# Advancing a state-space scan four time steps at a time instead of two, in a two-layer decoder trunk

## The chip, the cores and the metric

The kernel runs on one core of a Trainium2 chip. The metric is the time of one execution on the device in microseconds. The core has a matrix engine (TensorE, PE in the profile; its weight loads have a row of their own, PEld), a vector engine (VectorE, DVE), a scalar engine (ScalarE, ACT), GpSimd (POOL) and SyncE (SP), which here issues the loads. Each engine takes its instructions in the order of its own queue, and they wait for one another by semaphores. Matmuls write PSUM; everything else lives in SBUF.

## The reference

Batch 1, 256 positions, model width 2048, float32. Layer 0 normalises x, projects it, and splits the result into `xa`, `ga` (1024 channels each) and `zb`, `gb` (2048 and 1024). The part that matters here is the state-space mixer on `xa`: 64 groups of 16 channels, each with 64 complex states.

```python
    ab_re = mag * jnp.cos(li * dt)
    ab_im = mag * jnp.sin(li * dt)
    ...
    bu_re = jnp.einsum('blgh,gph->blgp', uf, bb_re)
    bu_im = jnp.einsum('blgh,gph->blgp', uf, bb_im)
    ...
    _, _, h_re, h_im = lax.associative_scan(combine, (a_re, a_im, bu_re, bu_im), axis=1)
    y = (jnp.einsum('blgp,ghp->blgh', h_re, c_re.astype(f32))
         - jnp.einsum('blgp,ghp->blgh', h_im, c_im.astype(f32))
         + d_skip.astype(f32)[None, None] * uf)
```

So h(t) = a h(t-1) + bb u(t) for each state, and y(t) = Re(C h(t)) + d u(t). After it come a GELU, a gated linear unit (`w_glu`), and a product with silu(`ga`). The other half of layer 0 is a spatial gate on `zb`, `gb`; both halves go through `w_out0`, and x is added. Layer 1 is differential attention with its own projections; a last normalisation follows.

## The kernel before

**Weights and main matmuls.** All weight matrices are cut into 140 chunks of 512 rows by 512 columns. SP loads them in a fixed order, written out by hand (`stream`), three buffers ahead. Each chunk is split in two exact parts: ACT writes the rounded part `wh` (line 82, the helper for all ACT work), DVE the rest `wl` (line 61, the helper for elementwise work on two tensors), again with three buffers. Three matmuls (hi by hi, hi by lo, lo by hi) take the place of one: `gemm_t` with 512 moving columns (lines 208 to 210), `gemm_c` with 256 (lines 221 to 224). Splits and the evacuation of a finished result are marked high priority. A planner that simulates engines in time orders the rest, in general by the order in which the program states it; the order of SP alone is kept as written. Main results have two PSUM buffers; the side work has one of two banks (`side2`) and two of one bank (`side1`, lanes 0 and 1).

**The state-space side work.** Groups are taken in pairs, so that 32 input channels and 128 states (2 x 64) belong together; there are 32 pairs. Time is taken two steps at a time: h(t+1) = a^2 h(t-1) + (a bb u(t) + bb u(t+1)), so 128 block steps remain of 256 positions. The steps are these:
- `ssm_params`: from the parameters dt, |a|, the phase, a (`ab`), the input factor (`fc`), its product with a (`fa`), |a|^2 (`r2`) and the powers of the unit rotation.
- `e_tables(half)`: for 16 pairs, a table E of the rotation's powers, 128 columns, by doubling.
- `ssm_consts`: `bbr` (the input matrices bb and a bb), `cA` and `cN` (output matrices C a and C), spread by masked copies into zeroed tiles, for all 32 pairs at once; and `pk0`, the direct path from u(t) to y(t), added to a diagonal of d (`diag_skip`, on POOL) in `intra`.
- `ssm_bT`: the input matrices transposed by TensorE (`pbt`) into `bT`.
- `ssm_set(S)`, 8 sets of 4 pairs: W = bT u (line 568), turned back by E (`f`), scanned on DVE with the real factor r2 (line 584, one scan for each pair and part), turned forward (`b`, then `hst`), and y from `hst` through `cA` and `cN` (line 606) plus `intra` (line 598); for every second set GELU into `yaf`.

These are generators: `run_side` advances them between chunks of the `v` matmuls, the constants run before `xa`, the sets of a half follow `xa` of that half in program order, ahead of `u`, `gb` and `ga`. Their result is needed at `glu`, after the first half of `w_out0` (`eo`). `yaf` is split there into `yah` and `yal`.

**In float32**, a matmul stands in the profile as two records, each with a weight load of its own; a transpose as one.

Of the kernel before, what the change touches and what calls it, by code (L numbers as in the profile page):

```python
# [29 lines left out]
def hybrid_trunk_kernel(ctx: ExitStack, tc: tile.TileContext, xT, xtok, w_in0, w_glu, w_out0,  # L30
# [53 lines left out]
    def rsqrt_mean(name, ss, n, eps, post=None):  # L84
        """(ss / n + eps) ** -0.5: an integer first guess, a cubic step and a Newton step."""
# [32 lines left out]
    # ---------------------------------------------------------------- weight stream  # L118
# [37 lines left out]
    def split(upto, before=None):  # L156
        """hi = the weight rounded to float32r, lo = the exact rest."""
# [80 lines left out]
    # ---------------------------------------------------------------- start: x^T, norm  # L238
# [51 lines left out]
    # the norm's factor: per token on partitions, and as a row on every partition  # L290
# [31 lines left out]
    # ---------------------------------------------------------------- SSM constants  # L322
# [34 lines left out]
    cst = {}  # L357

    def ssm_params():
# [7 lines left out]
        r2 = p32("r2")  # L367
        mul(r2, mag, mag)
        cst["r2"] = r2
# [50 lines left out]
        fa = p32("fa", 64).rearrange("p (c m) -> p c m", c=2)  # L420
        mul(t1, fc[:, 0, :], ab[:, 0, :])
        mul(t2_, fc[:, 1, :], ab[:, 1, :])
        sub(fa[:, 0, :], t1, t2_)
        mul(t1, fc[:, 0, :], ab[:, 1, :])
        mul(t2_, fc[:, 1, :], ab[:, 0, :])
        add(fa[:, 1, :], t1, t2_)
        cst.update(ab=ab, fc=fc, fa=fa, ep=ep)
        yield
        # powers of exp(i * 2 phi): 1, 2, 4, ..., 64
        pw = []  # L430
        prev = ep
        for j in range(7):
# [5 lines left out]
            e = p32(f"pw{j}", 64).rearrange("p (c m) -> p c m", c=2)  # L438
# [5 lines left out]
        cst["pw"] = pw  # L444
        yield

    bbr = [None, None]

    def sc16(ap):
        return ap.unsqueeze(2).to_broadcast([128, 32, 16])  # L450

    def diag_skip():
        intra = t8(11, "intra", [128, 16, 128])
        for i in range(16):
            G.tensor_scalar(out=intra[:, i, :], in0=ident, scalar1=dq[:, i:i + 1], scalar2=None, op0=ALU.mult)
        cst["intra"] = intra

    def masked(dst, src):
        for gg in range(2):
            r = slice(gg * 64, gg * 64 + 64)  # L460
            act(dst[r, :, gg * 16:gg * 16 + 16], src[r], AF.Copy)

    def ssm_consts():
        for c in range(2):
            bbr[c] = t8(7 + c, f"bbr{c}", [128, 32, 2, 32])
            G.memset(bbr[c], 0.0)
        cA = t8(9, "cA", [128, 2, 32, 32])
        cN = t8(10, "cN", [128, 2, 32, 32])
        G.memset(cA, 0.0)
        G.memset(cN, 0.0)  # L470
        cst.update(cA=cA, cN=cN)
        b_re, b_im, c_re, c_im = (bct[:, i] for i in range(4))
        for gg in range(2):
            r = slice(gg * 64, gg * 64 + 64)
            h = slice(gg * 16, gg * 16 + 16)
            act(cN[r, 0, :, h], c_re[r], AF.Copy)
            act(cN[r, 1, :, h], c_im[r], AF.Copy, scale=-1.0)
        yield
        for key, z_re, z_im, o_re, o_im, sign in (
                ("fc", b_re, b_im, bbr[0][:, :, 1, :], bbr[1][:, :, 1, :], 1.0),  # L480
                ("fa", b_re, b_im, bbr[0][:, :, 0, :], bbr[1][:, :, 0, :], 1.0),
                ("ab", c_re, c_im, cA[:, 0], cA[:, 1], -1.0)):
            s = cst[key]
            m1 = t4(f"m1{key}", [128, 2, 32, 16])
            m2 = t4(f"m2{key}", [128, 2, 32, 16])
            mul(m1[:, 0], z_re, sc16(s[:, 0, :]))
            mul(m1[:, 1], z_im, sc16(s[:, 1, :]))
            mul(m2[:, 0], z_im, sc16(s[:, 0, :]))
            mul(m2[:, 1], z_re, sc16(s[:, 1, :]))
            sub(m1[:, 0], m1[:, 0], m1[:, 1])  # L490
            if sign > 0:
# [3 lines left out]
            masked(o_re, m1[:, 0])  # L495
            masked(o_im, m2[:, 0])
            yield
        # K0 = Re(C bb) and the skip, as one matrix per two pairs
        intra = cst["intra"]
        pk0 = side1("pk0", [128, 16, 32])  # L500
        for i in range(16):
            for q in range(2):
                P = i * 2 + q
                o = pk0[q * 64:q * 64 + 32, i, :]
                PE.matmul(o, bbr[0][:, P, 1, :], cN[:, 0, P, :], start=True, stop=False)
                PE.matmul(o, bbr[1][:, P, 1, :], cN[:, 1, P, :], start=False, stop=True)
        for q in range(2):
            r = slice(q * 64, q * 64 + 32)
            o = intra[r, :, q * 64:q * 64 + 32]
            add(o, pk0[r], o)  # L510
        yield

    def ssm_bT():
        bT = [t8((14, 6)[c], f"bT{c}", [128, 16, 128]) for c in range(2)]
        for c in range(2):
            for g in range(4):
                p = side1(f"pbt{c}{g}", [128, 4, 128], g % 2)
                for ct in range(4):
                    i = g * 4 + ct
                    src = bbr[c][:, 2 * i:2 * i + 2].rearrange("p q j h -> p (q j h)")  # L520
                    PE.matmul(p[:, ct, :], src, ident, start=True, stop=True, is_transpose=True)
                act(bT[c][:, g * 4:g * 4 + 4, :], p, AF.Copy)
            yield
        cst["bT"] = bT

    U2 = t8(12, "U2", [128, 2, 2, 4, 128])
    etab = {}

    def e_tables(half):
        E = big.tile([128, 2, 16, 128], F32, name=f"E{half}", tag="e")  # L530
        etab[half] = E
        hs = slice(half * 16, half * 16 + 16)
        pw = cst["pw"]
        V.memset(E[:, 0, :, 0:1], 1.0)
        V.memset(E[:, 1, :, 0:1], 0.0)
        V.tensor_copy(out=E[:, :, :, 1:2], in_=pw[0][:, :, hs].unsqueeze(3))
        for k in range(1, 7):
            n = 1 << k
            for q in range(2):
                ph = slice(q * 8, q * 8 + 8)  # L540
                es = E[:, :, ph, 0:n]
                sh = [128, 8, n]
                m = [t4(f"em{half}{k}{q}{i}", [128, 2, 8, 64])[:, :, :, 0:n] for i in range(2)]
                for i in range(2):
                    a = pw[k][:, i, half * 16 + q * 8:half * 16 + q * 8 + 8].unsqueeze(2).to_broadcast(sh)
                    for c in range(2):
                        mul(m[i][:, c], es[:, c], a)
                o = slice(n, 2 * n)
                sub(E[:, 0, ph, o], m[0][:, 0], m[1][:, 1])
                add(E[:, 1, ph, o], m[0][:, 1], m[1][:, 0])  # L550
# [574 lines left out]
```

## Time and profile before

| | |
|---|---|
| median of 3 runs | 888.91 us (888.35 to 889.16) |
| profiled execution, its span | 887.3 us |
| PE / DVE / ACT / POOL busy | 871.7 / 666.3 / 448.8 / 38.3 us |
| first `xa` result evacuated (`xs`) | 101.7 us |
| last `yaf` copy starts | 307.4 us |
| first matmul of `glu` | 335.0 us |
| granted TensorE clock, mean | 0.996 |

The span runs from the first to the last instruction of one profiled execution; the times of the runs are the device's for a whole execution, so a little more than the span (here 1.6 us between the median and the span, which are of different executions). Busy shares are averages over stages; a PE that is busy can still be slower than its best, since the ends of matmuls are modelled and overlap the next.

### The profile page before, as it was taken

The page shows a single profiled execution, that of the slowest core. Times are in us where ns is not written, and L with a number is a line of the kernel's source. Part 1 is how long each engine was busy: PE and PEld are TensorE (multiplying, and loading weights), DVE is VectorE, ACT ScalarE, POOL GpSimd, SP SyncE. Part 2 cuts the span into 40 slices and gives each one's busy share as a digit, 9 for nine tenths or more (in the row PEclk, how much of TensorE's full clock was granted, in tenths as well). Part 3 has the DMA queues.
Part 4 walks back from the last instruction along what each step waited for, and adds up shares of the span by engine and source line. Part 5 has one row for each costly group of instructions (what it writes and reads, how often), then busy time and mean ns, then how long its engine had stood idle before and what let it go on. Part 6 is the DMA issues. An engine that isn't in the chain of part 4 may idle for free.

```text
span 887.3 us, 14016 instructions
## 1 busy us (share of the span) xinstructions
PE 871.7 (98%) x5598; PEld 778.4 (88%) x5598; DVE 666.3 (75%) x1219; ACT 448.8 (51%) x623; POOL 38.3 (4%) x47
## 2 busy tenths in 40 slices
PE   9999999999999999999999999999999999999995
PEld 7799978788999789889988999889988998888895
DVE  8999869999988866567866677666767577665773
ACT  6563862455334645565345543554346544554551
POOL 7110000000000100000000000000000000000000
PEclk9999999999999999999999999999999999999998
DMA  8965452234534655455554545554454455555542
GB/s 306 379 243 191 143 190 96 96 120 166 190 114 141 259 185 176 170 195 202 180 182 160 188 145 190 191 190 152 181 190 171 165 188 196 183 189 190 178 155 96
DMA packets 25985, 160.24 MB, mean 181 GB/s; under 512 B 2880, under 2 KB 4160, under 8 KB 7744
## 3 DMA queue, kind: packets, MB, share of 16 engines
q1 hardware_dynamic: 25344, 156.20, 49.2%
q0 software_dynamic: 576, 3.15, 1.0%
q8 instruction: 44, 0.72, 0.3%
q14 instruction: 21, 0.17, 0.1%
HBM read 157.24 MB, written 2.10 MB: 180 GB/s over the span
## 4 chain that ended last, share of the span: by engine, by line
PE 90%; DVE 7%; ACT 1%; issue 1%; DMA 0%; DVEq 0%; ACTq 0%
PE v L209 5%; PE v L210 5%; PE v L208 5%; PE k L224 3%; PE q L221 3%; PE k L223 3%; PE k L221 3%; PE q L224 3%; PE q L223 3%; PE g L210 3%; PE g L209 3%; PE g L208 3%; PE od L209 2%; PE od L208 2%; PE od L210 2%; PE ga L221 2%
## 5 line engine op out<-in xcount | busy, mean ns | idle before, releaser
L82 ACT ACTIVATE wh<-wr 128x1024 fp32r<-128x1024 f32 (+1 forms) x276 | 288.7, 1047 | 356.0 <-PE v L210 64.0
L61 DVE TENSOR_TENSOR wl<-wr,wh 128x1024 fp32r<-128x1024 f32 (+1 forms) x276 | 331.8, 1205 | 142.2 <-ACT wh L82 141.4
L224 PE MATMUL k<-h2h,wl 128*128 128x256 f32 x256 | 72.8, 284 | 0.0
L221 PE MATMUL q<-h2h,wh 128*128 128x256 f32 x256 | 72.7, 284 | 0.0
L223 PE MATMUL q<-h2l,wh 128*128 128x256 f32 x256 | 72.7, 284 | 0.0
L224 PE MATMUL q<-h2h,wl 128*128 128x256 f32 x256 | 72.6, 284 | 0.0
L221 PE MATMUL k<-h2h,wh 128*128 128x256 f32 x256 | 72.4, 283 | 0.0
L223 PE MATMUL k<-h2l,wh 128*128 128x256 f32 x256 | 72.4, 283 | 0.0
L209 PE MATMUL v<-wl,h2h 128*128 128x512 f32 x128 | 50.8, 397 | 0.0
L209 PE MATMUL g<-wl,h2h 128*128 128x512 f32 x128 | 50.3, 393 | 0.0
L210 PE MATMUL g<-wh,h2l 128*128 128x512 f32 x128 | 50.1, 391 | 0.0
L210 PE MATMUL v<-wh,h2l 128*128 128x512 f32 x128 | 50.0, 390 | 0.0
L208 PE MATMUL v<-wh,h2h 128*128 128x512 f32 x128 | 50.0, 390 | 0.0
L208 PE MATMUL g<-wh,h2h 128*128 128x512 f32 x128 | 49.9, 390 | 0.0
L224 PEld LDWEIGHTS k<-h2h,wl 128*128 128x128 f32 x256 | 49.1, 192 | 0.1
L221 PEld LDWEIGHTS q<-h2h,wh 128*128 128x128 f32 x256 | 49.1, 192 | 0.2
L221 PEld LDWEIGHTS k<-h2h,wh 128*128 128x128 f32 x256 | 49.1, 192 | 0.0
L223 PEld LDWEIGHTS k<-h2l,wh 128*128 128x128 f32 x256 | 49.1, 192 | 0.0
L223 PEld LDWEIGHTS q<-h2l,wh 128*128 128x128 f32 x256 | 49.1, 192 | 0.0
L224 PEld LDWEIGHTS q<-h2h,wl 128*128 128x128 f32 x256 | 49.1, 192 | 0.0
L209 PE MATMUL od<-wl,oh 128*128 128x512 f32 x96 | 37.6, 392 | 0.0
L208 PE MATMUL od<-wh,oh 128*128 128x512 f32 x96 | 37.5, 391 | 0.0
(331 smaller groups left out, 2182.8 us busy)
## 6 DMA issues: line engine op xcount, KB each, us to landing
wr<-in_w_in_dram SPq DMA_DIRECT2D x100, 1024.0 KB, 4.8
wr<-in_w_out_dram SPq DMA_DIRECT2D x32, 1024.0 KB, 4.8
wr<-in_w_glu_dram SPq DMA_DIRECT2D x4, 1024.0 KB, 4.7
wr<-in_w_in_dram SPq DMA_DIRECT2D x8, 256.0 KB, 4.5
wr<-in_w_in_dram SPq DMA_DIRECT2D x4, 512.0 KB, 7.9
xk<-in_xtok_dram SPq DMA_DIRECT2D x2, 1024.0 KB, 10.9
xr<-in_xtok_dram POOLq DMA_DIRECT2D x2, 1024.0 KB, 7.6
out_dram<-x SPq DMA_DIRECT2D x6, 256.0 KB, 2.6
```

Source lines behind the costliest of these rows:

```text
L61: (eng or V).tensor_tensor(out=o, in0=a, in1=b, op=op)
L82: A.activation(out=o, in_=i, func=f, **kw)
L208: PE.matmul(ps[:, t, :], hi[:, s], wh, start=first and a == 0, stop=False)
L209: PE.matmul(ps[:, t, :], hi[:, s], wl, start=False, stop=False)
L210: PE.matmul(ps[:, t, :], lo[:, s], wh, start=False, stop=last and a == len(ktiles) - 1)
L221: PE.matmul(ps[:, c, :], wh[:, s], hi, start=first and a == 0 and c % 2 == 0, stop=False, skip_group_check=True)
L223: PE.matmul(ps[:, c, :], wh[:, s], lo, start=False, stop=False, skip_group_check=True)
L224: PE.matmul(ps[:, c, :], wl[:, s], hi, start=False, stop=fin, skip_group_check=True)
```

## The change

Time is taken four steps at a time. With a^4 (`r4`) as the factor of the scan, 64 block steps remain. Each pair's four inputs of 32 channels fill all 128 rows (`U`), in the order of steps 3, 2, 1, 0. The input matrices are a^k bb for k = 0 to 3 (`bbr`, from `sB`), the output matrices C a^(i+1) for the four outputs i (`ccs`, from `sC`). The outputs come from the state with which a block begins (`hst`, whose first column stays zero) and from a block matrix `intra` of 128 rows by 128, made of the products C a^k bb (`pk`, `kx`, transposed to `kt`) and the diagonal d.

The sets become 4 of 8 pairs. E has 64 columns; one scan takes all 8 pairs of a part in a row of 512, with a factor table `R` that is zero at the first column of each pair. The constants are built for one set at a time (`ssm_bc(s)`, `ssm_mats(s)`): for set 0 where they stood before, for sets 1 to 3 between the sets. `bbr`, `ccs`, `intra` and `cN` are one tile each, written anew for each set; `bT` is a new tile in one place. Places change: `bbr` goes from places 7 and 8 to 9, `ccs` to 10, `intra` and `cN` with the factors to 11. The input copies of `xs` into `U` are 16 for each half, of 256 columns, where 8 of 512 were. `rsqrt_mean`, the main matmuls and layer 1 are the same; some comments are gone.

```diff
@@ ssm_params
-        r2 = p32("r2")
-        mul(r2, mag, mag)
+        r4 = p32("r4")
+        mul(r4, mag, mag)
+        mul(r4, r4, r4)
...
+        sB, sC = (ic[:, z:z + 256].rearrange("p (c k m) -> p c k m", c=2, k=4) for z in (1536, 1792))
+        def cmul(o, x, y, n):
+            yb = [y[:, c].unsqueeze(1).to_broadcast([128, n, 32]) for c in range(2)]
+            m = t2("cm", [128, 2, n, 32])
+            for c in range(2):
+                mul(m[:, 0], x[:, 0], yb[c])
+                mul(m[:, 1], x[:, 1], yb[1 - c])
+                (add if c else sub)(o[:, c], m[:, 0], m[:, 1])
+        V.tensor_copy(out=sC[:, :, 0], in_=ab)
+        V.tensor_copy(out=sB[:, :, 0], in_=fc)
+        cmul(sC[:, :, 1:2], sC[:, :, 0:1], ab, 1)
+        cmul(sC[:, :, 2:4], sC[:, :, 0:2], sC[:, :, 1], 2)
+        cmul(sB[:, :, 1:4], sC[:, :, 0:3], fc, 3)
...
-    def diag_skip():
-    def ssm_consts():
-    def ssm_bT():
...
+    bbr = t8(9, "bbr", [128, 2, 8, 4, 32])
+    ccs = t8(10, "cc", [128, 2, 8, 4, 32])
+    intra = ic[:, 0:1024].rearrange("p (m i h) -> p m i h", m=8, i=4)
+    cN = ic[:, 1024:1536].rearrange("p (c m h) -> p c m h", c=2, m=8)
...
+    def ssm_zero():
+        for z in (ic[:, 0:1536], bbr, ccs):
+            G.memset(z, 0.0)
...
     def masked(dst, src):
         for gg in range(2):
             r = slice(gg * 64, gg * 64 + 64)
+            act(dst[r, :, :, gg * 16:gg * 16 + 16].rearrange("p m k h -> p k m h"), src[r], AF.Copy)
+    def ssm_bc(s):
+        if not s:
+            ssm_zero()
+        ms = slice(s * 8, s * 8 + 8)
+        b_re, b_im, c_re, c_im = (bct[:, i, ms] for i in range(4))
+        for gg in range(2):
+            r, h = slice(gg * 64, gg * 64 + 64), slice(gg * 16, gg * 16 + 16)
             act(cN[r, 0, :, h], c_re[r], AF.Copy)
             act(cN[r, 1, :, h], c_im[r], AF.Copy, scale=-1.0)
+        sh = [128, 4, 8, 16]
+        for key, z_re, z_im, o in (("sB", b_re, b_im, bbr), ("sC", c_re, c_im, ccs)):
...
+            mul(m1[:, 0], z_re, f_re)
+            mul(m1[:, 1], z_im, f_im)
+            mul(m2[:, 0], z_im, f_re)
+            mul(m2[:, 1], z_re, f_im)
             sub(m1[:, 0], m1[:, 0], m1[:, 1])
...
+            masked(o[:, 0], m1[:, 0])
+            masked(o[:, 1], m2[:, 0])
             yield
+    def ssm_mats(s):
+        pk = side1(f"pk{s}", [128, 2, 128], 1)
+        for g in range(2):
+            for r in range(4):
+                for c in range(2):
+                    PE.matmul(pk[r * 32:r * 32 + 32, g], cN[:, c, g * 4 + r, :],
+                              bbr[:, c, g * 4 + r].rearrange("p k h -> p (k h)"), start=c == 0, stop=c == 1,
+                              skip_group_check=True)
+        kx = t2(f"kx{s}", [128, 2, 128])
+        act(kx[:, :, 32:128], pk[:, :, 32:128], AF.Copy)
+        for g in range(2):
+            stt(kx[:, g, 0:32], i32, d4[:, s * 2 + g:s * 2 + g + 1], pk[:, g, 0:32], ALU.mult, ALU.add)
+        yield
+        bT = t8(14, f"bT{s}", [128, 2, 8, 128])
         for c in range(2):
+            for g in range(2):
+                p = side1(f"pbt{s}{c}{g}", [128, 4, 128], g)
+                for r in range(4):
+                    PE.matmul(p[:, r, :], bbr[:, c, g * 4 + r].rearrange("p k h -> p (k h)"), ident,
+                              start=True, stop=True, is_transpose=True)
+                act(bT[:, c, g * 4:g * 4 + 4, :], p, AF.Copy)
             yield
+        kt = side1(f"kt{s}", [128, 8, 32], 1)
+        for g in range(2):
+            PE.matmul(kt[:, g * 4:g * 4 + 4].rearrange("p m h -> p (m h)"), kx[:, g], ident,
+                      start=True, stop=True, is_transpose=True)
+        for i in range(4):
+            k = 3 - i
+            for r0, n in ((0, 128),) if k == 0 else ((0, 64),) if k == 2 else tuple((r, 32) for r in range(0, 128 - 32 * k, 32)):
+                act(intra[r0 + 32 * k:r0 + 32 * k + n, :, i], kt[r0:r0 + n], AF.Copy)
+        yield
...
     def e_tables(half):
+        if not half:
+            E[0] = big.tile([128, 2, 32, 64], F32, name="E", tag="e")
...
-        for k in range(1, 7):
+        for k in range(1, 6):
...
+    def ssm_set(s):
...
+        W = side2(f"W{s}", [128, 2, 8, 64])
         for c in range(2):
+            for m in range(8):
+                PE.matmul(W[:, c, m, :], cst["bT"][:, c, m, :], U[:, s * 8 + m, :], start=True, stop=True)
+        R = t2(f"R{s}", [128, 8, 64])
+        r4 = cst["r4"][:, ms].unsqueeze(2)
+        act(R[:, :, 0:1], r4, AF.Copy, scale=0.0)
+        act(R[:, :, 1:64], r4.to_broadcast([128, 8, 63]), AF.Copy)
...
         for c in range(2):
+            gf = flat(g)[:, c]
+            V.tensor_tensor_scan(out=gf, data0=R.rearrange("p m t -> p (m t)"), data1=gf, initial=0.0,
+                                 op0=ALU.mult, op1=ALU.add)
...
+        sub(h[:, 0, :, 1:64], m1[:, 0, :, 0:63], m2[:, 1, :, 0:63])
+        add(h[:, 1, :, 1:64], m1[:, 1, :, 0:63], m2[:, 0, :, 0:63])
         yield
+        y = side1(f"y{s}", [128, 8, 64], 1)
+        for m in range(8):
+            PE.matmul(y[:, m, :], intra[:, m].rearrange("p i h -> p (i h)"), U[:, s * 8 + m, :],
+                      start=m == 0, stop=False, skip_group_check=True)
+        for m in range(8):
+            for c in range(2):
+                PE.matmul(y[:, m, :], ccs[:, c, m].rearrange("p i h -> p (i h)"), h[:, c, m, :],
+                          start=False, stop=c == 1, skip_group_check=True)
...
+        for q in range(2):
+            for i in range(4):
+                r = slice((qh * 2 + q) * 32, (qh * 2 + q) * 32 + 32)
+                o = ya["f"][r, half * 4:half * 4 + 4, :].rearrange("p c (t i) -> p c i t", i=4)[:, :, i, :]
+                act(o, y[i * 32:i * 32 + 32].rearrange("p (c q) t -> p q c t", q=2)[:, q], AF.Gelu_apprx_tanh)
...
     def ssm_half(half):
         if half:
             yield from e_tables(half)
+        for s in (2 * half, 2 * half + 1):
+            if s:
+                yield from ssm_bc(s)
+                yield from ssm_mats(s)
+            yield from ssm_set(s)
     side.append(ssm_params())
     side.append(e_tables(0))
-    side.append(ssm_consts())
+    side.append(ssm_bc(0))
...
-    for _ in ssm_bT():
+    for _ in ssm_mats(0):
         pass
...
             for q4 in range(4):
-                for j in range(2):
+                for j in range(4):
+                    r0 = (3 - j) * 32
...
```

## Rows read from the trace of the kernel before

**Rows 1.** The page, busy time of each engine, its share of the span, instructions
```profile
PE 871.7 (98%) x5598; PEld 778.4 (88%) x5598; DVE 666.3 (75%) x1219; ACT 448.8 (51%) x623; POOL 38.3 (4%) x47
```

**Rows 2.** The table of windows: us, then each engine's busy us, clock, DMA
```profile
100.00:200.00 100.00, 96.60 (x589) 79.69 (x588) 86.65 (x174) 52.41 (x69) 0.00 (x0) 1.00 0.35 123
200.00:310.00 110.00, 109.64 (x782) 98.07 (x781) 98.08 (x144) 53.18 (x60) 4.10 (x7) 1.00 0.48 172
310.00:870.00 560.00, 560.00 (x3459) 504.79 (x3458) 382.00 (x580) 280.33 (x407) 8.22 (x10) 1.00 0.50 178
```

**Rows 3.** Waits of PE: on whom, us in total, times, longest
```profile
PE v L209 <- DVE wl L61: 1.6, 2, 0.8
PE gb L208 <- ACT ut L82: 1.4, 1, 1.4
...
PE u L209 <- DVE wl L61: 0.8, 1, 0.8
PE pbt L521 <- ACT bT L82: 0.8, 1, 0.8
PE u L208 <- ACT ut L82: 0.5, 1, 0.5
```

**Rows 4.** Groups of PE: form, passes, busy us, mean ns
```profile
L568 PE MATMUL W<-U,bT 64*128 64x128 f32 x128 | 17.2, 281 | 0.0
L606 PE MATMUL y<-hst,cA 128*32 128x128 f32 x128 | 16.4, 274 | 0.0
```

**Rows 5.** Chain of waits, 90 to 310 us: start us, us, piece
```profile
99.26 0.59 PE pbt L521 x4
...
177.54 0.34 PE y L606 x2
...
179.66 1.88 PE y L606 x30
...
195.22 1.98 PE W L568 x16
...
202.87 0.89 PE y L598 x8
...
275.32 1.09 PE y L598 x8
```

**Rows 6.** Tile pk, line 506: ns min/median/max, first and last start us
```profile
L506 PE MATMUL pk<-cN,bbr x64: 196/196/217, 97.0 to 99.1; 128*32 128x32 f32 x64
```

**Rows 7.** Timeline at 419 us: start us, us, instruction
```profile
418.77 0.28 PE L224 MATMUL q<-h2h,wl 128*128 128x256 f32 x1
418.77 0.31 PEld L841 LDWEIGHTS plam<-lprod,ones 128*128 128x128 f32 x2
418.89 0.28 PE L841 MATMUL plam<-lprod,ones 128*128 128x2 f32 x2
419.00 0.19 PEld L221 LDWEIGHTS q<-h2h,wh 128*128 128x128 f32 x1
...
419.23 0.28 PE L223 MATMUL q<-h2l,wh 128*128 128x256 f32 x1
```

**Rows 8.** Groups of DVE: form, count, busy us, mean ns
```profile
L584 DVE TENSOR_TENSOR_SCAN f<-r,f 128x128 f32<-128x128 f32 x64 | 21.1, 401 | 0.0
...
L61 DVE TENSOR_TENSOR em<-E,pw 128x512 f32<-128x512 f32 x16 | 10.1, 683 | 0.0
```

**Rows 9.** Groups of ACT: form, count, busy us, mean ns
```profile
L82 ACT ACTIVATE U<-xs 32x512 f32<-32x512 f32 x16 | 10.5, 658 | 0.6 <-DVE xs L61 0.4
...
L82 ACT ACTIVATE x2s<-x 128x256 f32<-128x256 f32 x4 | 1.7, 417 | 14.6 <-DVE x L61 14.6
...
L82 ACT ACTIVATE bbr<-m1fc 64x512 f32<-64x512 f32 x2 | 1.2, 622 | 0.0
```

**Rows 10.** Tile yaf, its reader yal: ns min/median/max, first and last start us
```profile
L61 DVE TENSOR_TENSOR yal<-yaf,yah x2: 1220/1223/1226, 288.7 to 310.3; 128x1024 fp32r<-128x1024 f32 x2
```

**Rows 11.** Tile glu, its first matmuls, columns as in the group before
```profile
L221 PE MATMUL glu<-yah,wh x64: 277/283/283, 335.0 to 357.7; 128*128 128x256 f32 x64
```

More of the change, by code (lines that the diff above doesn't have):

```diff
@@ L443, in ssm_params @@
             prev = e
[L444 removed]
+        cst["pw"] = pw[1:]
         yield
[L447 to L456 removed]
+    bbr = t8(9, "bbr", [128, 2, 8, 4, 32])
+    ccs = t8(10, "cc", [128, 2, 8, 4, 32])
+    intra = ic[:, 0:1024].rearrange("p (m i h) -> p m i h", m=8, i=4)
+    cN = ic[:, 1024:1536].rearrange("p (c m h) -> p c m h", c=2, m=8)
+    d4 = const.tile([128, 8], F32, name="d4")
+    i32 = const.tile([128, 32], F32, name="i32")
+    def ssm_zero():
+        for z in (ic[:, 0:1536], bbr, ccs):
+            G.memset(z, 0.0)
+        for r in range(4):
+            q = r % 2
+            rows = slice(r * 32, r * 32 + 32)
+            act(d4[rows], dq[q * 64:q * 64 + 32].rearrange("p (g a) -> p a g", a=2)[:, r // 2], AF.Copy)
+            act(i32[rows], ident[rows, rows], AF.Copy)
     def masked(dst, src):
@@ L511, in ssm_consts @@
         yield
-    def ssm_bT():
-        bT = [t8((14, 6)[c], f"bT{c}", [128, 16, 128]) for c in range(2)]
+        bT = t8(14, f"bT{s}", [128, 2, 8, 128])
         for c in range(2):
[L516 to L522, printed above, removed]
+            for g in range(2):
+                p = side1(f"pbt{s}{c}{g}", [128, 4, 128], g)
+                for r in range(4):
+                    PE.matmul(p[:, r, :], bbr[:, c, g * 4 + r].rearrange("p k h -> p (k h)"), ident,
+                              start=True, stop=True, is_transpose=True)
+                act(bT[:, c, g * 4:g * 4 + 4, :], p, AF.Copy)
@@ L537, in e_tables @@
-        for k in range(1, 7):
+        V.memset(e[:, 0, :, 0:1], 1.0)
+        V.memset(e[:, 1, :, 0:1], 0.0)
+        V.tensor_copy(out=e[:, :, :, 1:2], in_=pw[0][:, :, hs].unsqueeze(3))
+        for k in range(1, 6):
             n = 1 << k
[L539 to L550, printed above, removed]
+            m = [t4(f"em{half}{k}{i}", [128, 2, 16, n]) for i in range(2)]
+            for i in range(2):
+                a = pw[k][:, i, hs].unsqueeze(2).to_broadcast([128, 16, n])
+                for c in range(2):
+                    mul(m[i][:, c], e[:, c, :, 0:n], a)
+            o = slice(n, 2 * n)
+            sub(e[:, 0, :, o], m[0][:, 0], m[1][:, 1])
+            add(e[:, 1, :, o], m[0][:, 1], m[1][:, 0])
@@ L551, in e_tables @@
             if k >= 4:
                 yield
[L553 to L575 removed]
+    ya = {}
@@ L608, in ssm_set @@
-        yield
-        if q == 1:
-            if "f" not in ya:
-                ya["f"] = t8(7, "yaf", [128, 8, T])
-            for qq in range(2):
-                for i in range(2):
-                    r = slice((qh * 2 + qq) * 32, (qh * 2 + qq) * 32 + 32)
-                    o = ya["f"][r, half * 4:half * 4 + 4, :].rearrange("p c (t i) -> p c i t", i=2)[:, :, i, :]
-                    act(o, y[qq * 64 + i * 32:qq * 64 + i * 32 + 32], AF.Gelu_apprx_tanh)
+        y = side1(f"y{s}", [128, 8, 64], 1)
@@ new lines, in ssm_set @@
+        for m in range(8):
+            PE.matmul(y[:, m, :], intra[:, m].rearrange("p i h -> p (i h)"), U[:, s * 8 + m, :],
+                      start=m == 0, stop=False, skip_group_check=True)
+        for m in range(8):
+            for c in range(2):
+                PE.matmul(y[:, m, :], ccs[:, c, m].rearrange("p i h -> p (i h)"), h[:, c, m, :],
+                          start=False, stop=c == 1, skip_group_check=True)
+        yield
+        if "f" not in ya:
+            ya["f"] = t8(7, "yaf", [128, 8, T])
@@ L621, in ssm_half @@
             yield from e_tables(half)
-        for s in range(4):
-            yield from ssm_set(half * 4 + s)
+        for s in (2 * half, 2 * half + 1):
[3 more added lines that the diff above has]
+            yield from ssm_set(s)
     side.append(ssm_params())
     side.append(e_tables(0))
-    side.append(ssm_consts())
+    side.append(ssm_bc(0))
     G.affine_select(out=bw, in_=bw, pattern=[[0, 8], [1, 128]], compare_op=ALU.is_ge,
```

138 lines of the change are left out of this document (33 added, 105 removed).

## The prediction, written before the changed kernel was run

> **What bounds the kernel now.** I read the engines' line of the page first: TensorE (PE) is busy 871.7 us of a span of 887.3, 98%, VectorE (DVE) 75%, ScalarE (ACT) 51% [rows 1]. Averages hide stages, so the table of windows comes next: from 310 to 870 us PE is busy throughout; from 100 to 310 us, where the state space runs, PE is still busy 206.2 of 210 while DVE is busy 184.7 [rows 2]. TensorE's granted clock is 1.00, its 2.4 GHz level, in all three stretches. So DVE is nearly full there too, and the question is whether PE waits for it. The view of waits answers: the listed waits of PE for other engines are 1.6, 1.4, 0.8, 0.8 and 0.5 us, together 5.1 us in the whole run [rows 3]. I take the end to be set by the sum of PE's own passes. Relief of DVE or ACT can win back some 5 us at most; each microsecond of new PE work in layer 0 costs one.
>
> **PE, the work that goes and that comes.** A float32 matmul stands in the trace as two passes, each with its own weight load (a transpose as one). A set of matmuls is priced from the chain of waits, where a run of passes has its real length, since one matmul's listed duration overlaps its neighbours.
>
> Before: the input matmuls W are 8 sets of 16 passes [rows 4] at 1.98 us a set [rows 5]: 15.8 us. The outputs from `cA` and `cN` are 128 passes each with 32 output rows [rows 4]; they lie in pairs on different columns of the array, 30 passes in 1.88 us [rows 5], so 0.063 us each: 16.0 us for 256, and 0.2 us for each of 8 entries (two passes at the head of a set took 0.34 us): 17.6. The within-block matmuls `intra` are 32 passes, 8 in 0.89 to 1.09 us [rows 5]: 3.9. The matmuls of `pk0` are 128 passes in one stretch from 97.0 to 99.1 us [rows 6]: 2.1. The 32 transposes `pbt` are 8 groups at 0.59 [rows 5]: 4.7. Sum 44.1 us.
>
> After: the columns that move fall from 128 to 64 for W, `intra` and `ccs`, and all of these fill 128 columns of weights. The trace has no such pass with 64 columns, so I bound it. From above: W with 128 columns, 1.98/16 = 0.124 us. From below: the two passes of `plam` move 2 columns against 128 columns of weights, in the middle of a steady stream. The weight loads start at 418.77 for its two, and the next at 419.00: 0.115 us for each pass, though hardly anything moves; the matmuls say the same, since from the main pass at 418.77 to the second one after the pair, at 419.23, lie four passes, 0.115 each [rows 7]. Between 2 columns at 0.115 and 128 at 0.124 I take 0.115: a full weight load sets the price, and halving the moving columns saves nothing. That is the step on which the forecast stands.
> - W: 4 sets x 8 pairs of groups x 2 parts = 64 matmuls, 128 passes: 14.7, with 0.2 us for each of 4 entries 15.5.
> - `ccs`: 64 matmuls, 128 passes, 128 rows out where 32 were: 15.5.
> - `intra`: 32 matmuls, 64 passes, and 0.1 for each of 4 entries: 7.8.
> - `pk`: 64 matmuls of 32 output rows on four places, now with 128 columns: 128 passes. At the pair price 0.063: 8.0. Should four run beside one another, half of it, 4.0; should none, 0.115 each, 14.7. I take the pairs, the nearest row.
> - `pbt`: 64 transposes, 16 groups at 0.59: 9.4. `kt`: 8 passes and entries: 1.3.
>
> Sum 57.5 us, 13.4 more than before (9.4 to 20.1 by `pk` alone). The number of state steps has halved, but passes that load a full 128 columns of weights rise from 192 to 392, and passes of 32 columns fall from 384 to 128. All of these stand in PE's one queue with the main matmuls; nothing hides them.
>
> The Trainium skill speaks against this price: "TensorE: Matmul & The Clock Gate", section "Back-to-back issue gap", lists about 60 cycles for 1 to 64 columns as the gap of a single matmul, about 25 ns. By it the 320 passes of 64 columns would cost some 8 us rather than 37. The same section says that the figure leaves out the weight load, and the rows on `plam` show what the load does here.
>
> **DVE.** A column of an elementwise operation costs 0.683/512 = 1.33 ns [rows 8]. Goes: 4 sets replace 8 of the same size, 6,144 columns each: 65 us to 33. The 64 scans of 128 columns, 21.1 us [rows 8], become 8 of 512, each between an elementwise operation of that size, 0.68, and four old scans, 1.60; I take 1.2, so 9.6. The tables' columns halve, 24,192 to 11,904: 32 us to 16. Comes: the constants, 18 operations of 512 columns and two additions (14 us), become 48 (33), with 8 small ones for `kx` and some 18 for the powers, an estimated 5. In all 132 to 97, a relief of 35 us (25 of them after the input `xa`, since three quarters of the constants move there) that PE does not wait for. It gains nothing beyond the 5.1 us; if my reading is wrong, see the second rival.
>
> **ACT.** `U` is copied in 32 pieces of half the size where 16 were; a piece was 0.658 [rows 9]. The masked copies, 0.62 each [rows 9], go from 12 to 32, the `bT` copies from 8 to 16, `yaf` from 16 to 32 smaller ones; `R`, `kx` and 24 small copies to `intra` are new. I estimate 35 to 72 us. These stand in ACT's queue with the weight splits that PE needs. What hides them is ACT's idle half, 47.6 of 100 us and 56.8 of 110 [rows 2], and three buffers of weights. The place to watch is the block of `U` copies: the wait of 0.8 at u L209 comes after it, and 16 copies at 0.417, as another ACT operation of 256 columns takes [rows 9], are 6.7 us where 8 at 0.658 were 5.3, so up to 1.4 us more. Against that `ut` no longer shares a place with `bbr`, and the wait of u L208, 0.5, should go. New waits of PE for `kx`, the masks and the two small PSUM tiles have no row; between none and, for each of three later sets, the 0.8 that `pbt` lost once in the old order [rows 3] twice over, up to 5. I take a net of zero, within -5 to +6.
>
> **POOL, SP.** 16 multiplications by the diagonal leave POOL; its memsets now all wait for the squares of x, long before use. SP's weight stream keeps its order; `bct` only stays longer in its place.
>
> **The sum.** 887.3 + 13.4 = 900.7 us of span. The median of the runs lies 1.6 us over the profiled span: 902.3, stated as 902.
>
> **Rivals.**
> 1. *The columns set the price.* If a pass of 64 columns costs half of 0.112, the 320 passes cost 18 us, not 37: 13.4 - 19 = -5.5, some 883 us. It decides from 320 x = 37 - 13.4, at 0.074 us a pass; below that the kernel is faster. For it: with 32 columns of weights, 32 moved columns cost 2.1/128 = 0.016 us a pass in `pk0` and 128 cost 0.063 in `y` [rows 5, 6], so there the moved columns do set the price. Against it: those loads are a quarter as wide, and the `plam` pair has the full width.
> 2. *DVE sets the stage.* DVE is busy 98.1 of 110 us from 200 to 310 [rows 2]; if PE's busy time were stretched by waits that the view does not list, the 25 us that leave DVE there would come off and the added passes would hide in it: some 864. Against it: PE's waits [rows 3].
> 3. *The chain of sets ends too late.* `yal` is ready soon after 310.3 us and `glu` starts at 335.0 [rows 10, 11]: 23 us in hand. In the new order each of three later sets must build its own constants after the set before: masks (8 x 0.62), `bT` (4 x 0.59) and small copies are some 10 us of ACT, 20 with half of it taken; 60 us for three, less 25 from DVE, would end at 346, 12 us past the old start of `glu`. PE would wait there: some 914. Against it: PE reaches `glu` later as well, and DVE's part of the next set's constants needs nothing from the set before.
> 4. *The saving is eaten but no more*: `pk` runs four abreast (9.4) and every listed wait goes (-5): 893, still slower.
>
> **How the numbers follow.** My forecast, with rival 4 as its lower end, 0.75, from 892 to 911; rival 1, 0.08; rival 2, 0.05; rival 3, 0.12. Runs of this kernel differ by 0.1%, so a change of 0.2% (1.8 us) can be told. Rivals 1 and 2 give faster 0.13; between them and 892 lies no case but mixtures, 0.04 for the same, taken from the forecast and rival 2; the rest, 0.83, is slower. The range of 8 in 10 leaves out the two faster rivals and the far end of the late chain: 888 to 914.
>
> **What would show it.** Right: W, `intra` and `ccs` of the changed kernel with weight loads 0.11 apart; PE busy time up by some 13 us, nearly all of it before 335 us; DVE some 35 us less busy; layer 1 the same length. Wrong: 64-column passes closer than 0.075; PE waits that shrink or grow by over 6 us; an idle PE ahead of `glu`; `pk` with passes 0.115 apart.

## The result, and the profile after

The changed kernel takes 922.9 us (median of 4 runs, 922.38 to 923.36) beside 888.74 for the kernel before: a ratio of 1.0378 (1.0365 to 1.0391). It is slower, as forecast, but by 34 us where I had said 13; it lies 9 us above my range. The profiled span went from 887.3 to 920.7 us.

The page after, its line of busy times and the slices of PE and of its granted clock:

```profile
PE 883.7 (96%) x5542; PEld 792.3 (86%) x5542; DVE 627.8 (68%) x1098; ACT 501.4 (54%) x738; POOL 20.6 (2%) x30
...
PE   8999698989789999999999999999999999999996
...
PEclk9999799989889999999999999999999999999999
```

Against [rows 1], DVE lost 38.5 us, ACT gained 52.6, and PE has holes: apart from the last slice (a 5 in the kernel before), the slices with 6, 7 or 8 all lie ahead of 310 us. The windows show the same. First kernel after, then kernel before in the stretch where the two differ most (columns as in [rows 2]):

```profile
100.00:200.00 100.00, 90.89 (x526) 77.98 (x527) 67.21 (x94) 66.80 (x100) 0.00 (x0) 0.93 0.34 117
200.00:310.00 110.00, 100.48 (x721) 91.14 (x720) 72.10 (x97) 66.02 (x99) 4.12 (x7) 0.94 0.38 136
215.00:265.00 50.00, 41.45 (x252) 35.65 (x250) 29.90 (x38) 29.05 (x44) 0.00 (x0) 0.86 0.30 106
310.00:900.00 590.00, 590.00 (x3636) 531.66 (x3635) 397.67 (x583) 296.31 (x422) 7.49 (x9) 1.00 0.51 181
```

```profile
215.00:265.00 50.00, 50.00 (x383) 46.84 (x382) 47.70 (x69) 19.55 (x22) 0.00 (x0) 1.00 0.43 149
```

From 215 to 265 us PE ran 252 passes where it had run 383, and the granted clock was 0.50, its 1.2 GHz level ("half clock" below), for part of it. From 310 us on PE is full at clock 1.00, as it was [rows 2]. The whole loss lies where the state space runs: the first matmul of `glu` starts at 368.4 us where it started at 335.0, and from there to the end both kernels take 552.3 us.

The waits of PE (on whom, us in total, times, longest), to be set beside [rows 3]:

```profile
PE xa L221 <- ACT wh L82: 8.3, 1, 8.3
PE pk L516 <- ACT bbr L82: 6.4, 1, 6.4
PE u L208 <- ACT ut L82: 2.3, 1, 2.3
PE s L715 <- ACT bT L82: 2.2, 1, 2.2
```

**Where the 33 us are.** I split the time from PE's first to its last matmul by the distance from one pass's start to the next: what a pass of its kind takes at the full clock, what the half clock adds, and the rest as waiting (short switches between kinds stay with the passes). This is worked out from all records of the trace, with the same rule for every kernel. Another threshold for what counts as waiting moves up to some 2 us between the waits and the half clock of this table, and 0.3 in the other columns.

| us | main passes | state-space passes | other | half clock | waits | all |
|---|---|---|---|---|---|---|
| before | 790.8 | 43.1 | 34.9 | 0.0 | 8.1 | 876.9 |
| after | 788.5 | 46.7 | 34.9 | 8.1 | 32.1 | 910.3 |

The forecast's +13.4 is +3.6 for the passes, or +1.3 with the 2.3 that main passes won. What I had taken as zero is +24.0 of waits and +8.1 of clock. The two longest waits make 14.7 us of those 32.1; none of the rest is over 2.5.

**The two long waits, read in ACT's queue.** ACT's timeline of the kernel after, at the wait of `xa` (PE idle from 94.3 to 102.6 us) and at the wait of `pk` (247.2 to 253.6):

```profile
88.38 1.06 ACT L82 ACTIVATE wh<-wr 128x1024 fp32r<-128x1024 f32 x1
89.46 7.42 ACT L82 ACTIVATE U<-xs 32x256 f32<-32x256 f32 x11
96.91 1.24 ACT L82 ACTIVATE vt<-vt,vnb,vrs 128x1024 f32<-128x1024 f32 x1
98.18 3.32 ACT L82 ACTIVATE U<-xs 32x256 f32<-32x256 f32 x5
101.52 2.00 ACT L82 ACTIVATE wh<-wr 128x1024 fp32r<-128x1024 f32 x2
...
247.24 5.03 ACT L82 ACTIVATE yaf<-y 32x256 f32<-32x256 f32 x8 [2.46 <-PE y L619]
252.28 1.27 ACT L82 ACTIVATE bbr<-m1sB 64x512 f32<-64x512 f32 x2
```

Between two weight splits (`wh`) stand 16 copies of `U` and a `vt`, 12.0 us; PE ran out of split weights. Later eight copies of `yaf`, 5.0 us, stand ahead of the masks that `pk` needs. The copies cost what I had not thought (min/median/max ns, first and last start):

```profile
L82 ACT ACTIVATE U<-xs x32: 644/658/682, 89.5 to 187.3; 32x256 f32<-32x256 f32 x32
...
L82 ACT ACTIVATE yaf<-y x32: 607/626/657, 138.4 to 295.2; 32x256 f32<-32x256 f32 x32
```

A copy of 256 columns costs as much as one of 512 did (0.658, [rows 9]). The source of `U` now takes every fourth column, where it took every second.

**Why PE had nothing else to do.** In the kernel before, the spatial gate and `gb` filled PE between the sets. In the kernel after they come late; rows of the tiles `s` and `ga` of the kernel after (the copies `gt` start at 259.9 us, before at 202.9):

```profile
L715 PE MATMUL s<-vt,bw x32: 272/275/553, 261.8 to 277.3; 128*128 128x128 f32 x32
```

```profile
L221 PE MATMUL ga<-hh,wh x128: 278/283/364, 268.4 to 324.5; 128*128 128x256 f32 x128
```

and the same rows of the kernel before:

```profile
L700 PE MATMUL s<-vt,bw x32: 270/275/275, 133.4 to 179.4; 128*128 128x128 f32 x32
```

```profile
L221 PE MATMUL ga<-hh,wh x128: 277/283/388, 223.7 to 288.3; 128*128 128x256 f32 x128
```

By the program text, `R` and `kx` of every set take the three buffers of `t2` that `gt` uses, and `pbt` the PSUM place (lane 0 of `side1`) that `s` uses; all sets stand ahead of them in program order, so `s` and `gt` get their places only when the last set has given them back.

### The profile page after: what moved, and what is told of

It reads as the page before. It is cut to its first block, busy times and chain, and to the rows that moved or that the text cites. A ratio compares the mean times of both kernels' runs of the same rounds, so it can differ in the third digit from the quotient of the medians.

```text
span 920.7 us, 13887 instructions
## 1 busy us (share of the span) xinstructions
PE 883.7 (96%) x5542; PEld 792.3 (86%) x5542; DVE 627.8 (68%) x1098; ACT 501.4 (54%) x738; POOL 20.6 (2%) x30
## 4 chain that ended last, share of the span: by engine, by line
PE 78%; ACT 5%; DVE 4%; issue 1%; DVEq 0%; ACTq 0%
PE k L224 3%; PE q L221 3%; PE k L223 3%; PE k L221 3%; PE q L224 3%; PE q L223 3%; PE v L209 3%; PE g L210 3%; PE g L209 3%; PE v L210 3%; PE v L208 3%; PE g L208 3%; PE od L209 2%; PE od L210 2%; PE od L208 2%; PE gb L209 2%
## 5 line engine op out<-in xcount | busy, mean ns | idle before, releaser
L221 PE MATMUL xa<-hh,wh 128*128 128x256 f32 x128 | 37.2, 291 | 8.3 <-ACT wh L82 8.3
L224 PE MATMUL xa<-hh,wl 128*128 128x256 f32 x128 | 37.2, 292 | 1.1 <-DVE wl L61 1.1
```

Of the source, the lines that this page charges most:

```text
L221: PE.matmul(ps[:, c, :], wh[:, s], hi, start=first and a == 0 and c % 2 == 0, stop=False, skip_group_check=True)
L224: PE.matmul(ps[:, c, :], wl[:, s], hi, start=False, stop=fin, skip_group_check=True)
```

## The experiments

The first four kernels separate the passes from the copies; 5, 6 and 8 try to cure the waits, 7 tests the price of a pass, and the last three the order. Ratios are to the kernel before, run on the same chip.

**1. The changed kernel with neighbouring columns.** `U` is read and `yaf` written without a stride, so the state space sees other time steps; all counts and sizes stay.

```diff
-  ....rearrange("p c (t j) -> p c j t", j=4)[:, :, j, :]   # U
+  ....rearrange("p c (j t) -> p c j t", j=4)[:, :, j, :]
-  ....rearrange("p c (t i) -> p c i t", i=4)[:, :, i, :]   # yaf
+  ....rearrange("p c (i t) -> p c i t", i=4)[:, :, i, :]
```

> The changed kernel, but the ACT copies into U read, and those into yaf write, neighbouring columns instead of every fourth (the values are those of other time steps; everything else is the same). Theory A (a 256-column ACT copy that takes every fourth column costs as much as 512 columns at every second, 0.66 us, and 16 of them in a row hold back the weight splits behind them, so PE waits 8.3 us and loses its clock): U and yaf copies fall from 0.658 and 0.626 to about 0.4 us, the U block from 10.7 to 6.5 us, the longest PE wait from 8.3 to about 4, time about 908 to 914. Rival B (the price of such a copy is set by its 32 rows or per instruction, not by the step between columns): copies stay at 0.63 to 0.66 and the time at 922 to 924.

Measured: 911.62 us, 1.0242 (1.0219 to 1.0265), 11.3 less than the changed kernel and as theory A had it. The copies in this kernel:

```profile
L82 ACT ACTIVATE U<-xs x32: 412/414/417, 89.2 to 179.6; 32x256 f32<-32x256 f32 x32
```

```profile
L82 ACT ACTIVATE yaf<-y x32: 356/376/378, 134.7 to 284.3; 32x256 f32<-32x256 f32 x32
```

Its waits of PE:

```profile
PE pk L516 <- ACT bbr L82: 4.5, 1, 4.5
PE xa L221 <- ACT wh L82: 4.3, 1, 4.3
```

The stride alone, of the reads for `U` and the writes of `yaf` together, costs 0.24 to 0.25 us a copy and 11 us of the time. The 0.417 that the forecast took is the price without a stride.

**2. Every second `U` copy on DVE.**

```diff
-                    act(o, src, AF.Copy)
+                    if j % 2:
+                        V.tensor_copy(out=o, in_=src)
+                    else:
+                        act(o, src, AF.Copy)
```

> The changed kernel, but every second copy into U runs on DVE instead of ACT (8 of 16 for each half). Theory A (the length of the block of copies in ACT's queue makes PE's longest wait, 8.3 us, and the clock falls because of it): the ACT block falls to about 5.3 us, the wait at xa falls below 2 us, no stretch of half clock near 100 us, time about 908 to 912. Rival C (the added passes of PE make the difference and the waits are only where it shows): time stays within 3 us of 922.9.

Measured: 920.82 us, 1.0375 (1.0335 to 1.0415): no gain, a miss for theory A, which said 908 to 912. The wait it aimed at did shrink, and others took its place:

```profile
PE pk L516 <- ACT yaf L82: 7.5, 2, 5.2
PE y L619 <- DVE hst L61: 3.5, 2, 3.3
...
PE xa L221 <- ACT wh L82: 1.7, 1, 1.7
```

PE won 6.6 us early and lost most of them later, at the chain of the sets. The time is the one that rival C gave, but not for its reason: passes cost 3.6 us by the table above.

**3. The kernel before, W cut in two.** Each W matmul of 128 columns becomes two of 64; nothing else changes.

```diff
-                PE.matmul(W[:, c, ct, :], ..., U2[rows, half, qh, ct, :], ...)
+                for z in (slice(0, 64), slice(64, 128)):
+                    PE.matmul(W[:, c, ct, z], ..., U2[rows, half, qh, ct, z], ...)
```

> The kernel before, but each of the 64 matmuls W with 128 moving columns is cut into two with 64: 256 passes instead of 128, the same columns in all. If a full load of 128 weight columns sets the price (0.112 us a pass at any number of columns up to 128): 128 passes more at 0.112 = 14.3 us, time about 902 to 904. If the moved columns set it: 0 to 2 us more, 889 to 891.

Measured: 916.8 us, 1.0299 (1.0261 to 1.0336), more than the 902 to 904 of the theory of the weight load. By the split, state-space passes went from 43.1 to 57.4 us, waits stayed (8.1 to 9.0), and the half clock took 14.1. In the chain (start, us), 32 passes of W with 64 columns, at the full clock, with 0.116 each:

```profile
142.94 3.71 PE W L569 x32
...
164.43 3.71 PE W L569 x32
```

So the price that the forecast rests on is right: a pass with half the columns costs 0.116 where one with 128 cost 0.124. What I had not foreseen stands in the windows (the column after POOL is the granted clock):

```profile
160.00:168.00 8.00, 8.00 (x73) 6.78 (x72) 7.97 (x15) 3.54 (x5) 0.00 (x0) 1.00 0.39 134
168.00:171.40 3.40, 3.40 (x10) 2.66 (x10) 3.30 (x5) 1.06 (x1) 0.00 (x0) 0.50 0.00 0
198.70:205.60 6.90, 6.90 (x24) 5.91 (x24) 6.74 (x21) 0.00 (x0) 0.00 (x0) 0.51 0.00 0
```

Towards the end of five of the eight sets of 32 such passes, or right behind them, with PE busy throughout, the clock fell to its 1.2 GHz level; three (from 125.8, 142.9 and 152.6 us) had no such fall, and one more fall (185.1) came behind a wait of 2.3 us. The loss differs from run to run: the four runs took 910.4 to 918.5 us, the fastest at a mean clock of 0.988, the others at 0.979 or 0.980.

**4. The kernel before, `U` in 32 copies of every fourth column.** The columns stand in another order of time.

```diff
-                    act(U2[...], src, AF.Copy)                        # 512 columns, every second
+                    for z in range(2):
+                        act(U2[..., z * 64:z * 64 + 64], src_z, AF.Copy)   # 256, every fourth
```

(`src_z` is part z of the source, every fourth column.)

> The kernel before, but each of the 16 ACT copies into U2 with 512 columns is cut into two of 256 that read every fourth column (the values stand in another order of time): 16 copies for each half of xa as in the changed kernel, and nothing else of the change. Theory A (the copies cost 0.66 us each whatever their number of columns, and their block in ACT's queue starves PE): the block is 10.5 us, PE waits 4 to 8 us more near 105 us and perhaps near 195, with clock lost, time 895 to 903. Rival B (price by columns, 0.33 to 0.42 us each): block 5.3 to 6.7 us, time 888 to 891.

Measured: 897.58 us, 1.0095 (1.008 to 1.011), 8.4 us more, as theory A had it; a copy took 0.646. The wait stands here at `u`, and the clock was half from 117.0 to 123.8 us:

```profile
PE u L208 <- ACT wh L82: 4.3, 1, 4.3
```

The copies alone, in a kernel otherwise unchanged, cost more than half of what the forecast gave to the passes.

**5. The 32 masked copies on DVE.** The sums write straight into the masked places.

```diff
-            sub(m1[:, 0], m1[:, 0], m1[:, 1])
-            masked(o[:, 0], m1[:, 0])            # two ACT copies
+            for gg in range(2):                  # rows r, places d0 of one group
+                sub(d0, m1[r, 0], m1[r, 1])
...
```

> The changed kernel, but the 32 masked copies of the constants (0.63 us each on ACT) are gone: DVE's last addition or subtraction writes the two halves into their places itself (32 operations on 64 rows for 16 on 128, and 4 negations). Theory A (ACT's queue makes PE late: strided copies, masks, GELUs ahead of the weight splits and of what TensorE needs next): ACT loses 20 us, the wait of pk for bbr (6.4 us) goes or falls below 2, the half clock behind it too, time 908 to 915. Rival D (the waits follow from the order in which the sets' constants hang on one another, whichever engine makes them): the wait of pk moves to DVE with 4 us or more, time 918 to 924.

Measured: 916.97 us, 1.0314 (1.0299 to 1.033); ACT fell to 482.0 us. The wait of `pk` fell from 6.4 to 3.2, but `pbt` now waited 2.5 for the masks on DVE and `gb` 4.5. The number lies between the theories (908 to 915 for A, 918 to 924 for rival D) and decides little; it is 5.9 us less than the changed kernel.

**6. Lighter ACT throughout.** The masks as in 5; DVE sorts `xs` by step as it writes it (so `U` reads neighbours) and sorts `yaf` at the end.

```diff
-            mul(xs, ps, rbc...)
+            for j in range(4):
+                mul(xs.rearrange("p c (j t) -> p c j t", j=4)[:, :, j], ps.rearrange("p c (t j) -> p c j t", j=4)[:, :, j], ...)
...
```

> The changed kernel with all three loads taken from ACT: masks as in e5_masks_dve; xs written by DVE already sorted by step, so that the U copies read neighbouring columns (0.41 us as in e1_contig); GELU writes neighbouring columns (0.38) and DVE sorts yaf once for each half before glu. The work of PE is that of the changed kernel. Theory A: PE's long waits fall from 24 us more than before to under 8, half clock under 15 us in all, time 890 to 900; what is left above 888.7 is the passes (+3.6 us by the trace of the changed kernel) and the rest of the waits. Rival C (PE's added passes cost 13 us as predicted): not below 902. Rival D: 905 or more, with the waits on DVE.

Measured: 906.18 us, 1.0188 (1.0173 to 1.0203), worse than the 890 to 900 that theory A gave, and as rival D had it: 905 or more, with the waits on DVE. The wait of `xa` was gone and ACT down to 465.9 us, yet PE starved in the same stretch, from 227.8 us, now for the result of the scan:

```profile
PE y L622 <- DVE hst L61: 5.0, 1, 5.0
```

```profile
215.00:265.00 50.00, 40.19 (x295) 37.77 (x294) 38.79 (x57) 20.42 (x39) 0.00 (x0) 0.80 0.15 48
```

With ACT busy 20 of these 50 us and DVE 39, I took it that what was missing was other work for PE. That led to kernels 9 to 11.

**7. The kernel before, its matmuls set abreast.** Not a test of the loss but of the price: a set takes two column tiles with both row places instead of four with one, so W alternates between the two halves of the rows (and two PSUM banks), and y between four column places.

```diff
-            for ct in range(4):
-                PE.matmul(W[:, c, ct, :], cst["bT"][c][rows, ...
+            for m in range(4):
+                ct, rows = cp * 2 + m // 2, slice(m % 2 * 64, m % 2 * 64 + 64)
+                PE.matmul(W[:, m % 2, m // 2, c, :], cst["bT"][c][rows, ...
...
```

> The kernel before, two steps at a time, but a set holds two column tiles of both row places instead of four of one: the passes of W alternate between rows 0-63 and 64-127 and between two PSUM banks, and those of y between four places of 32 output columns instead of two. The same passes, weights and columns. If passes on different places run beside one another as pk of the changed kernel did (four abreast): W from 15.8 to about 8 us and y from 16 to about 8 to 9.5, time 874 to 882. If W's rows do not overlap: 880 to 884. If two abreast is all that y gets: no change, 887 to 891. If the clock falls behind such bursts as in e3_before_w64: up to 8 us of that is lost.

Measured: 878.07 us, 0.9873 (0.9859 to 0.9888): it beats both kernels, by 11 us the one before. In the chain the same numbers of passes as in [rows 5] are nearly twice as fast:

```profile
251.69 1.09 PE W L568 x16
263.65 0.34 PE y L610 x2
264.65 1.04 PE y L610 x30
```

State-space passes fall from 43.1 to 28.7 us, and the clock is 1.00 throughout the state space. The Trainium skill has the rule, "TensorE: Matmul & The Clock Gate", section "Part 3: Packing small matmuls — row/col tiling": matmuls on different rows or columns of the array run at the same time. The trace agrees: 0.068 us a pass for W where it was 0.124, and 0.035 for y where it was 0.063. For W the rows and the PSUM banks changed together; no run tells their shares apart.

**8. The `U` copies without their high priority**, so that weight splits may pass them.

```diff
         with hp():
             xs = t4(f"xs{half}", [128, 4, T])
             mul(xs, ps, rbc.unsqueeze(1).to_broadcast([128, 4, T]))
-            for q4 in range(4):
-                for j in range(4):
+        for q4 in range(4):
+            for j in range(4):
...
```

> The changed kernel, but the copies into U do not have high priority: the planner may put weight splits between them. The work of every engine is the same. Theory A, in the form that the unbroken block counts: the wait at xa falls from 8.3 to under 3 us and the half clock near 100 us goes, time 908 to 916. Rival E (ACT's total work counts, not its order): 919 to 924.

Measured: 926.41 us, 1.0407 (1.039 to 1.0425), slower still. The wait of `xa` fell to 3.2, but `gb` waited 4.2, `pbt` 3.0 and `pk` 6.9, and the stretches at half clock grew from 31 to 37 us. A miss for theory A (908 to 916) and above what rival E gave (919 to 924); why the later waits grew I can't say.

**9. Places of their own.** `R` and `kx` in the buffers of `t4`, all `pbt` on PSUM lane 1.

```diff
-        kx = t2(f"kx{s}", [128, 2, 128])
+        kx = t4(f"kx{s}", [128, 2, 128])
...
-                p = side1(f"pbt{s}{c}{g}", [128, 4, 128], g)
+                p = side1(f"pbt{s}{c}{g}", [128, 4, 128], 1)
...
-        R = t2(f"R{s}", [128, 8, 64])
+        R = t4(f"R{s}", [128, 8, 64])
```

> The changed kernel, but the tiles R and kx rotate in the three larger work buffers (t4) instead of the three small ones (t2) that the evacuation of gb uses, and all transposes pbt go through lane 1, so that lane 0 of the small PSUM tiles is free for the spatial gate (s) and ybT. Work and durations are the same. Theory F (in program order the last set's R and kx hold the buffers of gt, and its pbt holds lane 0, so gb's PSUM and with it ga wait for the last set, and from 215 to 260 us PE has nothing else to run while the sets' chain makes it wait): s starts near 150 us instead of 262, ga near 235 instead of 268, the 6.4 us at pk and the half clock from 248 on go, waits 32 to about 18, time 902 to 911. Rival A (ACT's durations alone): 919 to 924, waits as before.

Measured: 914.04 us, 1.0277 (1.026 to 1.0294), 3 us above the 902 to 911 of theory F. What it said of the order came about: the gate came early again (`s` from 100.8 to 179.4 us), `gt` from 216.7, `ga` from 239.0 (268.4 in the changed kernel, 223.7 in the one before), and the wait of `pk` fell to 0.4. The first long wait stayed, now at `s`:

```profile
L221 PE MATMUL ga<-hh,wh x128: 277/283/583, 239.0 to 309.7; 128*128 128x256 f32 x128
```

```profile
PE s L715 <- DVE vt L61: 6.5, 1, 6.5
...
PE ga L221 <- ACT wh L82: 2.6, 1, 2.6
```

**10. Both: lighter ACT (6) and places of their own (9).**

> e6_act_light with the buffers of e9_own_buffers. Theory F together with A: the waits that e6 still had (19 us, 5.0 of them y for hst, 2.3 pk for yaf, at 227 to 243 us) fall to about 9, no half clock inside, time 889 to 895: the passes of four steps cost PE 1 to 4 us more and nothing else is left. Rival D (the chain of sets itself): 902 to 907 as e6_act_light.

Measured: 898.58 us, 1.0101 (1.0086 to 1.0116), 24.3 us less than the changed kernel but 4 us above the 889 to 895 that I expected. From 215 to 265 us PE is full again, and its waits are small:

```profile
215.00:265.00 50.00, 49.93 (x390) 46.61 (x389) 39.34 (x48) 27.04 (x40) 0.00 (x0) 1.00 0.42 148
```

```profile
PE u L208 <- ACT ut L82: 2.3, 1, 2.3
PE gb L208 <- DVE xs L61: 2.2, 1, 2.2
```

By the same split as above the rest over the kernel before is passes +3.0, waits +3.0 and half clock +2.9 us: 8.9 of 9.3. The cures alone gave 16.7 us (6) and 8.9 (9). The half clock stands here from 136.0 to 139.4 and 200.9 to 204.3 us, each time in or right behind one of the two waits shown. The sets' passes are those of the changed kernel.

**11. Only `R` and `kx` moved**, `pbt` left on both lanes.

> The changed kernel with only the first half of e9_own_buffers: R and kx in the larger work buffers, pbt on both lanes as it was. If the buffers of gt are the gate: gt at gb is early again, ga starts before 245 us, time 905 to 914 though s still waits for lane 0 until about 255 us. If lane 0 is the gate (ut must have s before gb's product can be formed, and the splits and PSUM behind it): no change, 919 to 924.

Measured: 922.05 us, 1.0361 (1.0336 to 1.0385), as the changed kernel. `ga` came earlier (from 248.1 us) but the spatial gate did not:

```profile
L715 PE MATMUL s<-vt,bw x32: 272/275/328, 270.0 to 285.1; 128*128 128x128 f32 x32
```

So the PSUM lane holds back `s`, and must go too: the time is the one that I had given for lane 0 as the gate. No run moved `pbt` alone.

## Why the prediction was right in direction and wrong in size

**The bound.** "The end is set by the sum of PE's own passes" held for the kernel before and stopped holding after the change. That is the error from which the rest follows: I had read that PE hardly waited (the view lists 6.6 us before; my 5.1 left out 1.1 at `psw` and 0.4 at `eo`; after, it lists 27.9), and took for granted that a kernel with 52.6 us more of ACT work (I had put it at 35 to 72) and another order of places would not wait either.

**The price of a pass: right.** The passes of 64 columns stand 0.106 to 0.107 us apart on average in the kernel after (W 13.6 us for 128, `ccs` and `intra` together 20.6 for 192), 0.117 in kernel 3; rival 1 needed less than 0.074. The 25 ns that the Trainium skill lists for a single matmul ("TensorE: Matmul & The Clock Gate", section "Back-to-back issue gap"), without the weight load as it says, is not the price of these passes, each of which brings its own.

**The sum of the passes: too large.** 57.5 us forecast, 46.7 measured: W 13.6 for 15.5, `ccs` and `intra` 20.6 for 23.3, `pbt` 6.8 for 9.4, `kt` 0.9 for 1.3, and `pk` 4.8 for 8.0, since its passes run four abreast (30 in 1.11 us at the full clock), the case I had given as the lower bound. The entries that I had added (0.2 us each) don't show in these distances. So the +13.4 that made the forecast were +3.6.

**The direction: right, but in good part by luck.** By the passes alone the kernel would have been slower by 1 to 4 us, at the edge of what I had said can be told; that it came out clearly slower is the work of the waits and the clock, which the forecast put at nothing. One sign of being right was met the same way: PE's busy time rose by 12.0 us where I had said 13, but the passes are at most 3.6 of it, and some 8 are passes drawn out by the half clock.

**DVE: right.** 38.5 us less busy, for a forecast 35, and no gain from it. Rival 2 is out, and rival 4 needed the waits to go.

**ACT: the step that failed.** "I take a net of zero, within -5 to +6" for the waits: measured +24.0, for PE waiting on ACT's queue and on the late sets. Two things were wrong in it.
- The price: "16 copies at 0.417" were 16 at 0.658, so the block is 10.5 us and with `vt` 12.0, not 6.7 us. I had the form of the operation right and its stride wrong; the row that I took (128x256 of `x2s`) reads neighbouring columns. Kernel 1 shows the stride by itself, 11.3 us with that of `yaf`; kernel 4 the copies of `U` by themselves, 8.4.
- The places: I asked what waits behind ACT's instructions, not which buffers the new tiles share with work that comes later in program order. Kernels 9 to 11 show that cause: 8.9 us alone, and with the lighter ACT 24.3 in all.

The two nearly add up: 16.7 (kernel 6) and 8.9 (kernel 9) make 25.6, and together they gave 24.3 (kernel 10). Alone or on top of the other, the lighter ACT is worth 15.5 to 16.7 us and the places 7.6 to 8.9, each good to some 2 us by the intervals; 9.3 us of the 34 remain. The parts of the lighter ACT go the same way: the strides 11.3 (kernel 1) and the masks 5.9 (kernel 5) make 17.2. Kernel 6 also moves work to DVE, so it does not price ACT's load alone. Smaller cures were given back in whole or nearly (2, 8, 11); each kernel is ordered anew by the planner.

**The clock: not in the forecast.** I took 1.00 throughout. It stood at half for 30.7 us of the kernel after, behind the wait of `xa` (97.8 to 108.0) and around the late sets:

```profile
97.80:108.00 10.20, 4.91 (x21) 4.61 (x22) 7.84 (x7) 7.71 (x10) 0.00 (x0) 0.50 0.29 101
...
247.90:258.20 10.30, 4.60 (x42) 3.42 (x42) 3.88 (x6) 10.05 (x17) 0.00 (x0) 0.50 0.18 76
```

Where PE had work there, it cost 8.1 us more. The fall at 247.9 came 0.7 us into the wait of `pk` and right behind 32 passes of `ccs`; which of the two brought it is not shown. In kernel 10 the same passes brought no fall without a wait.

**Rival 3** had the right suspect, sets that end too late, at the wrong place: `yal` is ready at 327.3 us and `glu` starts without a wait; the price was paid at 247 us, where PE had no other work, and it came from shared places: in kernel 9, with the same work in the chain, the wait of `pk` is 0.4 us.

## What to carry to other kernels

Price a copy by its access pattern as well, not by its count of columns alone: look for a row with the same stride before you halve a size. When a change adds tiles to shared rotating buffers, list who takes that buffer next in program order; an engine that never waited may have owed it to work that those buffers now hold back. And where small matmuls are priced by their weight loads, set them abreast on rows or columns of the array before you restructure the algorithm: that gave the only gain here.

## What the hardware showed unexpectedly

- ACT reads of every fourth float32 column cost 0.658 us for 256 columns, neighbouring ones 0.414; 512 columns at every second cost 0.658 too. Writes of `yaf` go alike, 0.626 against 0.376. DVE copied the same strided 256 in 0.380 (kernel 2). The Trainium skill, "Advanced Engine Details and Errata", section "Memory Cachelines", says that memory lines hold 16 bytes and that full speed needs two accesses to the same line; every second float32 column gives two, every fourth one. The ACT rows agree with it; whether DVE's 0.380 holds a penalty no run here shows.
- The granted clock fell not only behind waits but, in kernel 3, at five of eight sets of 32 passes with 64 columns, with PE busy throughout, to 0.50 for 3.4 to 6.9 us at a time; in kernel 10 it fell only in or behind two waits, of 2.3 and 2.2 us.
